# Low parts of split weights: a second use from DRAM, or a second subtraction

## The chip, the cores and the metric

One core of a Trainium2 chip (trn2) runs the whole program. The metric is the device time of one execution in microseconds (us), the median of several runs. The engines are named as the profile names them: PE is TensorE (PEld its weight loads), DVE is VectorE, ACT is ScalarE, POOL is GpSimd, and SP is SyncE, whose queue issues every DMA of this kernel.

## What is computed

Two token sequences, 512 and 256 long, 1024 channels wide, go through two layers that share one set of weights. In short:

```python
def encoder_trunk(x, mem, p):
    for l in range(2):
        xn = rmsnorm(x, p['norm_mix'][l])
        if l % 2 == 0:
            x = x + window_conv_mixer(xn, ...)               # layer 0: windowed attention and a gated conv
        else:
            x = x + rwkv7_bidir_time_mix(xn, ...)            # layer 1: six mixes of xn with its neighbours,
                                                             # r, k, v = products with three 1024x1024 weights,
                                                             # a forward and a backward recurrence over the tokens
        x = x + memory_cross_attention(rmsnorm(x), rmsnorm(mem), ...)
        gate, up = split(rmsnorm(x) @ p['ffn_wgu'][l])       # 1024 -> 2 x 2816
        x = x + (silu(gate) * up) @ p['ffn_wdown'][l]        # 2816 -> 1024
    return rmsnorm(x, p['norm_final'])
```

Everything is float32 and is held to float32's accuracy.

## The kernel before

**Split products.** A float32 matrix goes to TensorE as two parts in a rounded format (float32r): hi, which ScalarE rounds, and lo = value - hi. `mms` (L322 to L333) then issues three matmuls for every 128 rows of a weight: hi times the tokens' hi (L329), hi times their lo (L330), lo times their hi (L331). So every block of 128x128 weights that is used needs its hi and its lo in SBUF, in each place where it is used.

**Two ways to a split weight.** `wcols` (L250) serves the dense stages: one DMA brings 256 columns of up to 1024 rows as `wraw` (2 buffers, L262), ScalarE rounds each 128 columns into `whi` (L267) and VectorE subtracts into `wlo` (L268), 3 buffers each. `wtiles` (L276) serves the work in small pieces: a DMA brings 128 columns of 512 rows as `traw` (2 buffers, L287), ScalarE rounds into `thi` (L293), and the subtraction into `tlo` (L294, 3 buffers) is GpSimd's where the pieces run beside the scans, VectorE's elsewhere. One such piece of 4 x 128 rows is called a tile below; for 256 tokens TensorE makes 12 matmuls of it.

**The stages.** From about 760 us on: the last part of layer 0's feed-forward for the long sequence (`ffn` with `LATE`, hidden columns 8 to 21 of 22, by 128), then layer 1's r, k and v for the long sequence (`rwkv_in`, its inner function `full`), then, from 1278 us to about 2370 us, the recurrences (`mixer1_scan`). The recurrences are cut into 12 units; each unit is prepared (`prep`), has small triangular matrices inverted (`inverse`), is scanned (`scan`) and finished (`tail`): chains of small steps over TensorE, ScalarE, VectorE and GpSimd. They do not fill TensorE.

**The fill.** So dense work for the short sequence is woven in between: `fill` (L1388) makes, in order, the short sequence's hidden columns 8 to 21 of layer 0 (`ffn_small`, L391, with both its gate and up weights and its down weights), its low ranks (`small_low`), its v, k and r (`small_in`, L944), and then the keys and values of layer 1's memory and the output product (`mem_kv`, `rwkv_out`). The weights of `ffn_small` and of `small_in` are those that the dense stages used for the long sequence a few hundred us earlier; the weights of the other three are not.

**What sets the order.** A scheduler lays out the engines' queues at build time; each engine then runs its queue strictly in that order. Before the first scan, the fill's steps are placed beside `prep` and `inverse` by `weave`; inside a scan, `pour` releases some of the fill after a given matmul of the scan and not before:

```python
                todo[0] += rate[2 + u] / 24
                while todo[0] >= 1:
                    todo[0] -= 1
                    with tc.issue_after(last[0].ins):
                        next(fill, None)
```

SP's queue is in order too: a DMA that waits for its buffer holds up every DMA behind it, those of the scans included (`iok`, `ior`, `iov` at L1069, `w2r` at L1074, `v` at L1239).

Of the kernel before, what the change touches and what calls it, by code (L numbers as in the profile page):

```python
# [9 lines left out]
F32 = mybir.dt.float32  # L10
# [5 lines left out]
PSUM = bass.MemoryType.PSUM  # L16
# [9 lines left out]
# buffers of the dense layers' ring of big tiles  # L26
NBIG = 4
# how dense work is spread beside the scans (by step, before and after the long sequence's outputs are there)
FILL = ([1.2, 1.2] + [1.05] * 3 + [1.] * 3, [.9] * 2 + [1.] * 3 + [.5, 0.])
# rows of a weight between two points where the fill may pause, by tokens  # L30
PIECE = {256: 2, 512: 1, 768: 8}
# the hidden layer, by 128: the first layer's groups for all tokens and for the long sequence only, and the last layer's
# [5 lines left out]
class Net:  # L38
# [17 lines left out]
    def at(self, n):  # L56
        """The same, for tensors of n tokens."""
        f = copy.copy(self)
        f.W, f.seqs = n, ((0, n),)
        return f  # L60

    def sm(self, *shape):
        """A PSUM bank."""
        n = 1
        for s in shape:
            n *= s
        t = self.psm.tile([128, 512], F32, name="sm" if self.psm is not self.pmm else "mm")[:, :n]
        return t if len(shape) == 1 else t.rearrange("p (a b) -> p a b", b=shape[-1])
# [12 lines left out]
    def of(self, q):  # L81
        """The same, for one sequence."""
# [14 lines left out]
    def open_dense(self, small=3):  # L97
        """Pools for the dense layers."""
# [25 lines left out]
    def consts(self):  # L124
# [13 lines left out]
        # times the weights of the norm before  # L138
# [9 lines left out]
    # ---- residual stream, channel-major  # L148
# [8 lines left out]
    def rsqrt(self, v, n, eps, scale):  # L157
        """v [128, n] -> 1/sqrt(scale * v + eps), to float32's accuracy."""
# [17 lines left out]
    def spread(self, y, n):  # L176
        """y [128 tok, n token tiles] -> [128, n*128], the same row in every partition."""
# [12 lines left out]
    def square(self, m, x, acc=None, quick=False):  # L190
        """Adds the squares of x (channels 128*m on) per partition; quick: the last ones are left for rstd to add."""
# [12 lines left out]
    def rstd(self, acc, spread=True):  # L204
        """1/rms from the squares: in every partition, or (not spread) with the tokens on the partitions."""
# [22 lines left out]
    def split(self, src, g=None, tag="xs", bufs=16):  # L228
        """src (* g per channel) = hi + lo, both float32r."""
# [10 lines left out]
    def norm_in(self, name, l):  # L240
        """x*g split, and the squares for 1/rms (the products are scaled after)."""
# [6 lines left out]
    # ---- weights  # L248
    def wcols(self, w, r0, nk, c0, n):
        """Columns c0..c0+n of the rows r0..r0+128*nk of w, 128 at a time, as hi + lo by 128 rows."""  # L250
# [8 lines left out]
        for g0 in range(c0, c0 + n, W):  # L259
# [3 lines left out]
            for j in range(0, g, cw):  # L263
# [5 lines left out]
                for i in range(0, m, 128):  # L269
                    yield [(hi[:, k, i:i + 128], lo[:, k, i:i + 128]) for k in range(nk)]  # L270

    def wtiles(self, seq):
        """(hi, lo) of 128x128 blocks, of each (parts, rows[, factors of the rows]) of seq: 128 columns (in parts) of a
        matrix. Loads run ahead."""
# [3 lines left out]
        def load():  # L278
            for parts, nk, *scale in seq:
                for k0 in range(0, nk, 4):  # L280
# [8 lines left out]
                    for f in scale:  # L289
# [4 lines left out]
                    (nc.gpsimd if self.slots else nc.vector).tensor_sub(lo[:, :n], raw[:, :n], hi[:, :n].bitcast(F32))  # L294
# [8 lines left out]
    def abreast(self, ws, xs):  # L303
        """Some products of the same tokens, that take each of xs as it comes."""
# [6 lines left out]
    def mm(self, ps, w, xs, start=True, stop=True):  # L311
        """ps[out, tok] += w^T xs, in three passes."""
# [3 lines left out]
    def products(self, ps, pairs):  # L316
        """ps = the sum of a^T b over pairs (a, b), each in two parts, in three passes."""
# [17 lines left out]
    def ffn(self, l, given=None, groups=((0, 8), (8, 16), (16, 22)), keep=None, outs=None):  # L335
        """given: the norm's results, else they are left in normed. keep: gets the short sequence's hidden layer, which is not multiplied here."""
# [3 lines left out]
        pre = ahead(self.wcols(gu, 0, 8, c, 256), self.wcols(gu, 0, 8, DFF + c, 256))  # L340
# [8 lines left out]
        for h0, h1 in groups:  # L349
            hid = []  # L350
            for j in range(h0, h1, 2):
                if j != groups[0][0]:
                    pre = [self.wcols(gu, 0, 8, j * 128, 256), self.wcols(gu, 0, 8, DFF + j * 128, 256)]
# [27 lines left out]
            else:  # L381
                (self if keep is None else self.of(0)).ffn_down(l, h0, hid)

    def ffn_down(self, l, h0, hid):
        n = len(hid)
        for m, w in enumerate(self.wcols(self.a["ffn_wdown"][l], h0 * 128, n, 0, D)):
# [4 lines left out]
    def ffn_small(self, l, x, hid, part, h):  # L391
        """The same for few tokens, in small pieces, from tile h of the hidden layer on; what those before gave is in part.
        hid holds four tiles of the hidden layer."""
# [10 lines left out]
        for h0 in range(h, NH, 4):  # L404
            h1 = min(h0 + 4, NH)
            ws += [([gu[:, c:c + 128]], 8) for j in range(h0, h1) for c in (j * 128, DFF + j * 128)]
            ws += [([dn[h0 * 128:h1 * 128, c:c + 128]], h1 - h0) for c in range(0, D, 128)]
# [27 lines left out]
    # ---- cross-attention  # L435
    def mem_norm(self):
        """Both memories over their rms, to DRAM."""
# [17 lines left out]
    def mem_kv(self, l):  # L455
        """K [128 ch, 2*256] by 128 channels and V [128 tok, 4, 128] by 128 channels, of both memories, to DRAM."""
# [23 lines left out]
    def ca(self, l, kv):  # L480
# [3 lines left out]
        def load(h):  # L484
            """keys and values of a head, split"""
# [24 lines left out]
        def attend(h, st):  # L510
# [3 lines left out]
            def turn(p, t2):  # L514
                """keys on the partitions"""
# [62 lines left out]
    # ---- dilated-window attention and gated convolution  # L578
    def mixer0_tables(self, pool):
        """How many branches hold a pair of positions (by distance), and -1e30 where none does."""  # L580
# [25 lines left out]
    def mixer0(self):  # L606
# [23 lines left out]
        # the first products do not wait for the norm  # L630
# [26 lines left out]
        def turned(o):  # L657
            """values, token-major"""
# [10 lines left out]
        def attend(p, o):  # L669
# [3 lines left out]
            def turn(e, pT, hs, s0, t, n):  # L673
                """the probabilities of a tile of queries, keys on the partitions; values summed after two tiles"""
# [926 lines left out]
```

## Time and profile before

| what | us |
|---|---|
| median of 3 runs | 3186.92 |
| lowest and highest of them | 3182.41 and 3188.93 |
| the profiled execution, first to last instruction (its span) | 3179.3 |
| the profiled execution's own time | not listed apart from its span |
| busy in that span: PE | 2981.6 (94%) |
| DVE | 1948.5 (61%) |
| ACT | 1223.7 (38%) |
| POOL | 786.8 (25%) |

[...] Busy time of an engine includes time in which one of its instructions has begun and is held up. The stages differ, so shares over the whole span say little; the sections below go by stretches.

### The profile page before, as it was taken

What the parts mean: (1) busy time and instruction counts of PE and PEld (TensorE: products, weight loads), DVE (VectorE), ACT (ScalarE), POOL (GpSimd) and SP (SyncE); (2) the same over time, 40 slices, a digit from 0 to 9 for tenths busy, and PEclk for the clock granted to TensorE, in tenths of its full rate; (3) what the DMA queues carried; (4) which work ended last, traced back from release to release, by engine and by line L of the source; (5) the groups of instructions that cost most, each with busy time, mean ns of one, the idle gap of its engine ahead of it and who ended that gap; (6) DMA issues with size and microseconds to landing.
All of it is one profiled execution on the core that took longest, in us unless ns stands there. A gap on an engine that the chain in (4) does not pass through costs nothing. (4 is left out here: it accounts for less than half of the span.)

```text
span 3179.3 us, 49939 instructions
## 1 busy us (share of the span) xinstructions
PE 2981.6 (94%) x19984; PEld 2474.2 (78%) x19984; DVE 1948.5 (61%) x3492; ACT 1223.7 (38%) x2241; POOL 786.8 (25%) x753
## 2 busy tenths in 40 slices
PE   7999999999999899889888889999998999999997
PEld 6888788888888777677767767666677888888886
DVE  8678547464454684677697887666646564334244
ACT  3332434332222374454445565454435332122112
POOL 3112004020000201665466553343325120000001
PEclk9999999999999999889888998999999999999998
DMA  3123332112233435332232333222344211211211
GB/s 114 47 70 110 110 112 90 60 55 66 83 103 99 156 107 173 93 97 79 74 83 71 92 103 93 67 73 73 109 125 129 73 40 55 79 53 67 67 54 53
DMA packets 319880, 274.92 MB, mean 86 GB/s; under 512 B 37664, under 2 KB 283552, under 8 KB 319648
## 3 DMA queue, kind: packets, MB, share of 16 engines
q1 hardware_dynamic: 319648, 271.74, 27.0%
q8 instruction: 157, 2.57, 0.3%
q14 instruction: 75, 0.61, 0.1%
HBM read 234.46 MB, written 37.22 MB: 85 GB/s over the span
## 5 line engine op out<-in xcount | busy, mean ns | idle before, releaser
L329 PE MATMUL mm<-xs,whi 128*128 128x512 f32 x2128 | 752.6, 355 | 32.2 <-ACT whi L267 11.6
L330 PE MATMUL mm<-xs,whi 128*128 128x512 f32 x2128 | 753.4, 354 | 3.3 <-DVE xs L237 2.4
L331 PE MATMUL mm<-xs,wlo 128*128 128x512 f32 x2128 | 748.2, 352 | 3.8 <-DVE wlo L268 3.7
L267 ACT CAST whi<-wraw 128x1024 fp32r<-128x1024 f32 (+1 forms) x246 | 256.4, 1044 | 789.2 <-PE mm L330 757.3
L329 PEld LDWEIGHTS mm<-xs,whi 128*128 128x128 f32 x2128 | 403.1, 190 | 95.6 <-ACT whi L267 12.2
L201 POOL TENSOR_TENSOR acc<-acc,sq 128x768 f32<-128x768 f32 (+2 forms) x72 | 123.0, 1708 | 1412.7 <-ACT sq L198 1030.0
L331 PEld LDWEIGHTS mm<-xs,wlo 128*128 128x128 f32 x2128 | 401.6, 189 | 62.8 <-DVE wlo L268 5.5
L330 PEld LDWEIGHTS mm<-xs,whi 128*128 128x128 f32 x2128 | 402.9, 189 | 60.6 <-issue 3.3
L268 DVE TENSOR_TENSOR wlo<-wraw,whi 128x1024 fp32r<-128x1024 f32 (+1 forms) x246 | 314.0, 1279 | 158.7 <-ACT whi L267 150.8
L294 POOL TENSOR_TENSOR tlo<-traw,thi 128x512 fp32r<-128x512 f32 (+1 forms) x196 | 253.4, 1294 | 289.2 <-ACT thi L293 268.8
L330 PE MATMUL mm<-fb,thi 128*128 128x256 f32 (+1 forms) x720 | 242.6, 337 | 1.6 <-DVE fb L234 1.6
L329 PE MATMUL mm<-hid,whi 128*128 128x512 f32 (+1 forms) x528 | 186.9, 357 | 1.9 <-ACT hid L233 1.9
L330 PE MATMUL mm<-hid,whi 128*128 128x512 f32 (+1 forms) x528 | 188.2, 357 | 0.0
L329 PE MATMUL mm<-fb,thi 128*128 128x256 f32 x528 | 176.7, 335 | 11.0 <-ACT thi L293 10.9
L331 PE MATMUL mm<-hid,wlo 128*128 128x512 f32 (+1 forms) x528 | 186.7, 355 | 0.0
L331 PE MATMUL mm<-fb,tlo 128*128 128x256 f32 x528 | 164.0, 312 | 6.7 <-POOL tlo L294 6.5
L293 ACT CAST thi<-traw 128x512 fp32r<-128x512 f32 (+1 forms) x202 | 122.4, 608 | 121.1 <-PE mm L330 53.0
L369 DVE SCALAR_TENSOR_TENSOR u<-mm,rstd 128x768 f32<-128x768 f32 (+1 forms) x44 | 38.4, 873 | 211.6 <-PE mm L331 211.6
L1191 DVE TENSOR_TENSOR xr<-xr,lt 128x30 f32<-128x30 f32 (+4 forms) x360 | 156.0, 433 | 8.2
L330 PEld LDWEIGHTS mm<-fb,thi 128*128 128x128 f32 x720 | 152.7, 212 | 6.7 <-DVE fb L234 2.6
L1190 DVE TENSOR_TENSOR lt<-xr,lane 128x30 f32<-128x30 f32 (+4 forms) x360 | 149.5, 415 | 8.6
L389 DVE TENSOR_TENSOR x<-x,mm 128x512 f32<-128x512 f32 (+2 forms) x56 | 42.4, 762 | 175.9 <-PE mm L331 175.7
(366 smaller groups left out, 5995.5 us busy)
## 6 DMA issues: line engine op xcount, KB each, us to landing
wraw<-in_ffn_wgu_dram SPq DMA_DIRECT2D x44, 1024.0 KB, 4.9
wraw<-in_ffn_wdown_dram SPq DMA_DIRECT2D x23, 1024.0 KB, 5.0
traw<-in_ffn_wgu_dram SPq DMA_DIRECT2D x56, 256.0 KB, 3.0
wraw<-in_ab_w_in_dram SPq DMA_DIRECT2D x24, 512.0 KB, 3.6
wraw<-in_ca_wkv_dram SPq DMA_DIRECT2D x8, 1024.0 KB, 5.5
kvd<-kv SPq DMA_DIRECT2D x32, 256.0 KB, 2.0
kvr<-kvd SPq DMA_DIRECT2D x32, 256.0 KB, 2.6
wraw<-in_ca_wq_dram SPq DMA_DIRECT2D x8, 1024.0 KB, 5.2
```

The costliest lines, as they stand in the source:

```text
L201: nc.gpsimd.tensor_add(acc, acc, sq)
L267: nc.scalar.copy(hi[:, :, :m], raw[:, :, j:j + m])
L268: nc.vector.tensor_sub(lo[:, :, :m], raw[:, :, j:j + m], hi[:, :, :m].bitcast(F32))
L293: nc.scalar.copy(hi[:, :n], raw[:, :n])
L294: (nc.gpsimd if self.slots else nc.vector).tensor_sub(lo[:, :n], raw[:, :n], hi[:, :n].bitcast(F32))
L329: nc.tensor.matmul(ps[:, s0:s1], lhsT=wh, rhs=xh[:, s0:s1], start=start and k == 0, stop=False)
L330: nc.tensor.matmul(ps[:, s0:s1], lhsT=wh, rhs=xl[:, s0:s1], start=False, stop=False)
L331: nc.tensor.matmul(ps[:, s0:s1], lhsT=wl, rhs=xh[:, s0:s1], start=False, stop=stop and k == n - 1)
L369: nc.vector.scalar_tensor_tensor(u, pu, 0.5, rstd, op0=OP.mult, op1=OP.mult)
L389: self.nc.vector.tensor_add(self.x[m], self.x[m], ps)
L1190: nc.vector.tensor_mul(t, xr[:, m:, k:k + 1].to_broadcast([128, n, k]), ln[:, k:k + 1, 0:k].to_broadcast([128, n, k]))
L1191: nc.vector.tensor_add(xr[:, m:, 0:k], xr[:, m:, 0:k], t)
```

## The change

The first user of a weight keeps lo, the second user loads it:

- `wcols` gets a key (`keep`). With one, it issues a further DMA after each subtraction, from `wlo` to a DRAM tile `low` that belongs to that key and column. `ffn` passes a key where it is given the norm's results (the long sequence's columns 8 to 21: 28 gate and up columns and 16 down columns), `full` passes one for v, k and r (24 columns).
- `wtiles` takes such a tile as a third entry of a weight. With one, `tlo` is not computed: a DMA loads it from `low`. `ffn_small` and `small_in` pass them, for 56, 32 and 48 tiles. `thi` is rounded from `traw` as before.
- The other weights of the fill (low ranks, `mem_kv`, `rwkv_out`) keep GpSimd's subtraction.

```diff
+    def kept(self, key, nk):
+        if key not in self.lows:
+            self.lows[key] = self.lowd.tile([128, nk, 128], F32, name="low%d" % len(self.lows))
+        return self.lows[key]
-    def wcols(self, w, r0, nk, c0, n):
+    def wcols(self, w, r0, nk, c0, n, keep=None):
                 nc.vector.tensor_sub(lo[:, :, :m], raw[:, :, j:j + m], hi[:, :, :m].bitcast(F32))
                 for i in range(0, m, 128):
+                    if keep:
+                        nc.sync.dma_start(self.kept((*keep, (g0 + j + i) // 128), nk), lo[:, :, i:i + 128].bitcast(F32))
                     yield [(hi[:, k, i:i + 128], lo[:, k, i:i + 128]) for k in range(nk)]
...
-                    for f in scale:
+                    lows = scale if scale and len(scale[0].shape) == 3 else ()
+                    for f in () if lows else scale:
...
                     nc.scalar.copy(hi[:, :n], raw[:, :n])
-                    (nc.gpsimd if self.slots else nc.vector).tensor_sub(lo[:, :n], raw[:, :n], hi[:, :n].bitcast(F32))
+                    if lows:
+                        nc.sync.dma_start(lo[:, :n].bitcast(F32), lows[0][:, k0:k0 + n])
+                    else:
+                        (nc.gpsimd if self.slots else nc.vector).tensor_sub(lo[:, :n], raw[:, :n], hi[:, :n].bitcast(F32))
...
+        low = ("gu",) if given else None
...
-                (self if keep is None else self.of(0)).ffn_down(l, h0, hid)
+                (self if keep is None else self.of(0)).ffn_down(l, h0, hid, low and ("dn", h0))
...
-            wcs = self.wcols(a["rw_w" + c][0], 0, 8, 0, D)
+            wcs = self.wcols(a["rw_w" + c][0], 0, 8, 0, D, (c,))
...
-            col = lambda r, nk, m: ([w[r:r + 128 * nk, m * 128:m * 128 + 128]], nk)
+            col = lambda r, nk, m: ([w[r:r + 128 * nk, m * 128:m * 128 + 128]], nk, self.lows[c, m][:, r // 128:r // 128 + nk])
```

The order of the queues moves with it in three places.

SP's queue in the long sequence's feed-forward, where the raw weights are loaded (`wraw`) for `ffn`; before, a row "x8" is eight loads in a row:

```order
L262 DMA wraw<-in_ffn_wgu_dram 128x8x256 x6
L262 DMA wraw<-in_ffn_wdown_dram 128x8x256 x4
L262 DMA wraw<-in_ffn_wgu_dram 128x8x256 x8
L262 DMA wraw<-in_ffn_wdown_dram 128x8x256 x4
L262 DMA wraw<-in_ffn_wgu_dram 128x8x256 x6
```

and now, from the second of these rows on:

```order
L269 DMA wraw<-in_ffn_wdown_dram 128x8x256 x4
L269 DMA wraw<-in_ffn_wgu_dram 128x8x256 x2
L278 DMA low_7328<-wlo 128x1024
L278 DMA low_7336<-wlo 128x1024
L278 DMA low_7405<-wlo 128x1024
L269 DMA wraw<-in_ffn_wgu_dram 128x8x256
L278 DMA low_7440<-wlo 128x1024
L269 DMA wraw<-in_ffn_wgu_dram 128x8x256
```

One write of a low part stands in SP's queue for each column of 128, two for each load of raw weights, between the loads.

SP's queue where the fill begins beside the first unit's preparation, from the load of the scan's `v2` on, before:

```order
L1239 DMA v2_11924<-v00_8813 128x8x64
L287 DMA traw_10819<-in_ffn_wgu_dram 128x4x128
L287 DMA traw_10845<-in_ffn_wgu_dram 128x4x128
L287 DMA traw_10870<-in_ffn_wgu_dram 128x4x128
L287 DMA traw_10892<-in_ffn_wgu_dram 128x4x128
L287 DMA traw_10917<-in_ffn_wgu_dram 128x4x128
```

and now:

```order
L1255 DMA v2_12060<-v00_8901 128x8x64
L305 DMA tlo_10883<-low1_7336 128x512
L296 DMA traw_10955<-in_ffn_wgu_dram 128x4x128
L305 DMA tlo_10935<-low2_7405 128x512
L296 DMA traw_10981<-in_ffn_wgu_dram 128x4x128
L305 DMA tlo_10958<-low2_7405 128x512
L296 DMA traw_11006<-in_ffn_wgu_dram 128x4x128
L305 DMA tlo_10984<-low3_7440 128x512
```

Loads of raw and low parts alternate, and the low part of a tile stands behind the raw part of the tile after it. In the built program the load of `traw` waits for ScalarE's rounding (it waited for GpSimd's subtraction), and the load of `tlo` waits for the TensorE matmuls that used the buffer last.

TensorE's queue at the same place, the 6344th row of its order and those after it (`e` from `l0a` is a product of `prep`, L1057, now L1073; `g` are the first products of `inverse`, L1163; the others are the fill), before:

```order
L329 MATMUL mm_10916<-fb_10622,thi_10894 128x256
L330 MATMUL mm_10916<-fb_10622,thi_10894 128x256
L331 MATMUL mm_10916<-fb_10622,tlo_10895 128x256
L329 MATMUL mm_10916<-fb_10628,thi_10919 128x256
L330 MATMUL mm_10916<-fb_10628,thi_10919 128x256
L1057 MATMUL e_11048<-l0a_10535,w2r_10580 128x512
L1163 MATMUL g0_11193<-ar0_10838,bk0_10837 128x128
L1163 MATMUL g1_11194<-ar0_10838,bk0_10837 128x128
```

and now, in the same rows:

```order
L344 MATMUL mm_11052<-fb_10758,tlo_11031 128x256
L342 MATMUL mm_11052<-fb_10764,thi_11055 128x256
L343 MATMUL mm_11052<-fb_10764,thi_11055 128x256
L1073 MATMUL e_10978<-l0a_10671,w2r_10716 128x512
L344 MATMUL mm_11052<-fb_10764,tlo_11056 128x256
L342 MATMUL mm_11052<-fb_10770,thi_11055 128x256
L343 MATMUL mm_11052<-fb_10770,thi_11055 128x256
L344 MATMUL mm_11052<-fb_10770,tlo_11056 128x256
```

More of the fill stands in front of the first unit's products: the first `g` comes 58 rows later, and by the 80th matmul of the recurrences 130 more matmuls of the fill have gone before. By the 200th the difference is 6, and from there on the two orders hold the fill at the same places to within a tile or so.

## Rows read from the trace of the kernel before

**Rows 1.** The page: the span of the profiled execution.

```profile
span 3179.3 us, 49939 instructions
```

**Rows 2.** Stretches: us, then each engine's busy time (instructions), granted clock, DMA share, GB/s.

```profile
core 0: us, PE busy (x) PEld busy (x) DVE busy (x) ACT busy (x) POOL busy (x), PEclk, DMA share, GB/s
800.00:1000.00 200.00, 200.00 (x890) 165.78 (x889) 88.66 (x103) 49.86 (x58) 0.00 (x0) 1.00 0.29 94
```

**Rows 3.** Stretches of the recurrences: to the first scan's end, and while the fill shares weights.

```profile
1278.00:1425.00 147.00, 123.29 (x903) 101.86 (x902) 104.69 (x190) 72.76 (x147) 96.71 (x84) 0.89 0.31 90
...
1278.00:1920.00 642.00, 560.98 (x5183) 457.39 (x5184) 507.38 (x1079) 332.24 (x749) 369.57 (x385) 0.88 0.29 85
```

**Rows 4.** Waits of PE, 1278 to 1920 us: total us, times, longest us.

```profile
PE C L1254 <- DVE uv L1298: 20.1, 15, 3.4
PE C L1254 <- DVE S L1309: 14.7, 12, 2.5
PE mm L329 <- ACT thi L293: 6.0, 7, 1.4
...
PE mm L331 <- POOL tlo L294: 3.9, 2, 2.7
```

**Rows 5.** Groups of POOL, 1278 to 1920 us: xcount | busy us, mean ns | idle before it.

```profile
L294 POOL TENSOR_TENSOR tlo<-traw,thi 128x512 fp32r<-128x512 f32 (+1 forms) x144 | 186.6, 1298 | 148.0 <-ACT thi L293 129.7 <-PE C L1254 10.9 <-PE e L1023 3.5
```

**Rows 6.** Single lines of DVE, 1278 to 1920 us: ns min/median/max, first and last start.

```profile
L1191 DVE TENSOR_TENSOR xr<-xr,lt x210: 183/274/1396, 1343.4 to 1913.2; 128x30 f32<-128x30 f32 x14, 128x56 f32<-128x56 f32 x14, 128x78 f32<-128x78 f32 x14, 128x96 f32<-128x96 f32 x14
...
L1190 DVE TENSOR_TENSOR lt<-xr,lane x210: 174/271/1492, 1343.0 to 1913.0; 128x30 f32<-128x30 f32 x14, 128x56 f32<-128x56 f32 x14, 128x78 f32<-128x78 f32 x14, 128x96 f32<-128x96 f32 x14
...
L1298 DVE COPY uv<-C x47: 294/295/297, 1409.7 to 1915.7; 64x128 f32<-64x128 f32 x47
...
L1309 DVE TENSOR_TENSOR S<-C,Sd x72: 271/289/296, 1425.7 to 1918.6; 64x128 f32<-64x128 f32 x72
...
L169 DVE TENSOR_SCALAR rs_y<-rs_b x14: 163/172/1239, 1286.2 to 1877.5; 128x8 int32<-128x8 int32 x13, 128x2 int32<-128x2 int32 x1
```

**Rows 7.** Groups of DVE, 1278 to 1920 us: xcount | busy us, mean ns | idle.

```profile
L1191 DVE TENSOR_TENSOR xr<-xr,lt 128x30 f32<-128x30 f32 (+7 forms) x210 | 97.7, 465 | 4.6
L1190 DVE TENSOR_TENSOR lt<-xr,lane 128x30 f32<-128x30 f32 (+7 forms) x210 | 93.7, 446 | 4.7
```

**Rows 8.** Timeline around 1710 us: start us, duration us, engine, line [idle before].

```profile
1708.88 1.52 POOL L294 TENSOR_TENSOR tlo<-traw,thi 128x512 fp32r<-128x512 f32 x1
1709.19 1.24 DVE L169 TENSOR_SCALAR rs_y<-rs_b 128x8 int32<-128x8 int32 x1
...
1710.35 0.60 DVE L1309 TENSOR_TENSOR S<-C,Sd 64x128 f32<-64x128 f32 x2
...
1711.10 0.69 PE L1254 MATMUL C<-uv,G 64*64 64x64 f32 x8 [0.76 <-DVE S L1309]
```

**Rows 9.** DMA issues of the whole span: KB each, median us from issue to landing.

```profile
wraw<-in_ffn_wgu_dram SPq DMA_DIRECT2D x44, 1024.0 KB, 4.9
...
traw<-in_ffn_wgu_dram SPq DMA_DIRECT2D x56, 256.0 KB, 3.0
...
iok<-k SPq DMA_DIRECT2D x8, 256.0 KB, 2.7
```

**Rows 10.** Waits of SP's queue over the whole span.

```profile
SPq L262 <- DVE wlo L268: 1287.3, 119, 39.0
SPq L287 <- POOL tlo L294: 409.6, 144, 11.8
```

**Rows 11.** Timeline of PE: the first and the last of twelve matmuls of the fill.

```profile
1283.16 0.28 PE L329 MATMUL mm<-fb,thi 128*128 128x256 f32 x1
...
1284.46 0.28 PE L331 MATMUL mm<-fb,tlo 128*128 128x256 f32 x1
```

**Rows 12.** Lines that touch `traw`: ns min/median/max.

```profile
L293 ACT CAST thi<-traw x202: 389/618/637, 1083.5 to 2353.7; 128x512 fp32r<-128x512 f32 x97, 128x256 fp32r<-128x256 f32 x4
...
L287 SPq DMA_DIRECT2D traw<-in_ffn_wgu_dram x56: 367/368/539, 1234.3 to 1586.7; - x56
```

**Rows 13.** GpSimd's subtractions to the first scan's end: ns min/median/max.

```profile
L294 POOL TENSOR_TENSOR tlo<-traw,thi x42: 1262/1282/2187, 1283.1 to 1423.6; 128x512 fp32r<-128x512 f32 x42
```

More of the change, by code (lines that the diff above doesn't have):

```diff
@@ L339, in ffn @@
         c = 128 * groups[0][0]
-        pre = ahead(self.wcols(gu, 0, 8, c, 256), self.wcols(gu, 0, 8, DFF + c, 256))
+        low = ("gu",) if given else None
+        pre = ahead(self.wcols(gu, 0, 8, c, 256, low), self.wcols(gu, 0, 8, DFF + c, 256, low))
         first = None
@@ L352, in ffn @@
                 if j != groups[0][0]:
-                    pre = [self.wcols(gu, 0, 8, j * 128, 256), self.wcols(gu, 0, 8, DFF + j * 128, 256)]
+                    pre = [self.wcols(gu, 0, 8, j * 128, 256, low), self.wcols(gu, 0, 8, DFF + j * 128, 256, low)]
                 wg, wu = pre
@@ L381, in ffn, with ffn_down @@
             else:
-                (self if keep is None else self.of(0)).ffn_down(l, h0, hid)
-    def ffn_down(self, l, h0, hid):
+                (self if keep is None else self.of(0)).ffn_down(l, h0, hid, low and ("dn", h0))
+    def ffn_down(self, l, h0, hid, low=None):
         n = len(hid)
-        for m, w in enumerate(self.wcols(self.a["ffn_wdown"][l], h0 * 128, n, 0, D)):
+        for m, w in enumerate(self.wcols(self.a["ffn_wdown"][l], h0 * 128, n, 0, D, low)):
             ps = self.pmm.tile([128, self.W], F32, name="mm")
@@ L405, in ffn_small @@
             h1 = min(h0 + 4, NH)
-            ws += [([gu[:, c:c + 128]], 8) for j in range(h0, h1) for c in (j * 128, DFF + j * 128)]
-            ws += [([dn[h0 * 128:h1 * 128, c:c + 128]], h1 - h0) for c in range(0, D, 128)]
+            ws += [([gu[:, c:c + 128]], 8, self.lows["gu", c // 128]) for j in range(h0, h1) for c in (j * 128, DFF + j * 128)]
+            g0 = max(g for g, _ in LATE if g <= h0)
+            ws += [([dn[h0 * 128:h1 * 128, c:c + 128]], h1 - h0, self.lows["dn", g0, c // 128][:, h0 - g0:h1 - g0])
+                   for c in range(0, D, 128)]
         ws = self.wtiles(ws)
@@ L1516, in go @@
     n.xsave = [[dram.tile([128, s1 - s0], F32, name=f"xsave{q}{m}") for m in range(KT)] for q, (s0, s1) in enumerate(SEQS)]
+    n.lowd, n.lows = dram, {}
     n.consts()
```

## The prediction

> **What bounds the kernel now.** The page first, for the span: 3179.3 us [rows 1]; the median of the runs, 3186.92 us, lies 7.6 us above it, and the forecast is the median plus the sum below. Next the busy time by stretches, since one share over the whole span mixes stages. In the dense stage from 800 to 1000 us PE is busy 200.00 of 200 us at clock 1.00, for 890 matmuls, 0.225 us each [rows 2]: nothing but PE work counts there. From 1278 to 1920 us, where the recurrences run and the fill works with weights that were split before, it is different: PE is busy 560.98 of 642 us, so idle 81 us, and its clock is granted at 0.88, which costs about 0.12 x 642 = 77 us more [rows 3]. No other engine is full: DVE is busy 507 us (79%), POOL 370 us (58%). This stretch is a web of chains between engines, so I read the waits of PE there: the long ones end on DVE, 20.1 us on the copy L1298 and 14.7 us on the state sum L1309; on ScalarE's `thi` it waits 6.0 us and on GpSimd's `tlo` only 3.9 us [rows 4]. So the subtraction that goes is hardly waited for itself. What it does to DVE is the question.
>
> **GpSimd and VectorE hold each other up.** The group of L294 has 144 subtractions, 186.6 of POOL's 370 us, 1298 ns each [rows 5]. Single lines of DVE in the same stretch vary wildly: L1191 takes 183 to 1396 ns, L1190 174 to 1492, and L169, on 8 columns, 172 ns as a rule and 1239 at worst; the copy and the sum that read PSUM, L1298 and L1309, never leave 271 to 297 ns [rows 6]. The timeline shows one case: a subtraction runs from 1708.88 to 1710.40 us, L169 begins at 1709.19 and ends at 1710.43, just behind it, the state sum L1309 starts only then, and PE stands 0.76 us until it is done [rows 8]. That is the path by which a subtraction reaches the end of the kernel.
>
> **The change, part by part.**
>
> *Writes of the low parts*, 68 DMAs (60 of 512 KB, 8 of 384 KB) in the dense stages. I cost them at nothing. No engine computes for them; they read `wlo` behind the subtraction that makes it, which the next raw load in SP's queue waits for anyway (1287.3 us in all, over the span [rows 10]), so the queue stands where it stood. A raw load lands in 4.9 us [rows 9] and feeds two columns, 48 matmuls or 10.8 us of PE [rows 2]: that is the cover. If it were gone and each of the 34 raw loads concerned came 1 us late, it would cost 34 us.
>
> *Subtractions removed.* 136 go; four start before 1278 us, so 132 of the 144 in the group, 171 us or 46% of POOL's time in the stretch. The gain on DVE is bounded from rows. On L1191 the mean is 465 ns against a median of 274, on L1190 446 against 271 [rows 6, 7]: 210 x (0.191 + 0.175) = 77 us above the median on these two lines, and 46% of that is 36 us. This is the lower end; if the rest of DVE's 507 us suffered as these 191 us do, it would be 95 us, the upper end. I take 55 us, nearer the lower end, because the lines on PSUM do not suffer at all.
>
> [...]
>
> *What passes to the end.* Between nothing (DVE gets idle instead) and all of it. I take half, 28 us: DVE is the engine that PE waits for most, but not the only one. The clock: 81 us of idle PE go with 77 us of lost clock, so 28 us less idle could return up to 27 us; I take 14 us.
>
> *The start.* Before, a tile came every 147 / 42 = 3.5 us to the first scan's end [rows 3, 13], with PE idle 24 of 147 us. A raw buffer was then free only after landing (3.0 us), rounding (0.6) and subtraction (1.3); now after the first two, which with 0.4 us of issue is about 4 us for two tiles [rows 9, 12]. So the fill can run ahead, and the order now has 130 more of its matmuls, 130 x 0.118 = 15 us of PE [rows 11], in front of the 80th one of the recurrences. Bounds: 15 us gained if all of that falls into idle time, 15 us lost if the recurrences' chain is only pushed back and nothing returns. I take a gain of 4 us.
>
> *Loads of the low parts*, 136 DMAs on SP's queue, 132 x 0.37 = 49 us more of issue [rows 12], on a queue that waited 409.6 us for the subtraction [rows 10]. About 35 MB more in 642 us, 54 GB/s on top of 85, at a DMA share of 0.29 [rows 3]: no bound by itself. The new wait is the load's own: `tlo` has three buffers, so a load can go out when the matmuls of the tile three before are done, and needs 0.4 + 2.7 us (the landing of `iok`, also 256 KB with long rows [rows 9]), while two tiles of back-to-back fill last only 2 x 12 x 0.118 = 2.8 us [rows 11]. Behind a load that waits for PE stand SP's loads for the scans, and behind a matmul that waits for `tlo` stands the whole of PE's queue. Bounds: nothing where scan matmuls lie between the tiles (the mean distance is 642 / 144 = 4.5 us), 0.3 us for each of 132 tiles, 40 us, if all ran back to back. I take 7 us.
>
> Sum: 0 - 28 - 14 - 4 + 7 = -39 us, so **3148 us**.
>
> **The rivals.**
>
> *Late loads (slower).* The landing time in the sum is that of a lone load; now raw and low loads alternate. From 256 to 1024 KB the landing grows from 3.0 to 4.9 us [rows 9], 0.63 us for 256 KB, so two at once need 3.7 us against 2.8: 0.9 us short for each tile in a burst. At the start, where the new order has 40 tiles nearly in a row, that is 36 us on PE's queue, and with a fifth of the relief passing (11 us) the time is 3187 + 36 - 11 = 3212 us. It decides from about 3 us of issue to landing on. For it: the order has no slack for a longer landing. Against it: before, the raw buffers and a busy POOL made the fill slower still.
>
> [...]
>
> *Hidden anyway (no change).* The relief goes into DVE's own waits: what PE waits for, L1298 and L1309, runs at a constant time and waits in turn for PE and ScalarE. Then 3185 us. Against it: L1309 behind L169 in the timeline [rows 8].
>
> *All of it passes (much faster).* 55 us of relief and more, the 9.9 us on `thi` and `tlo`, and half of the clock's 77 us: 55 + 10 + 38 = 103 us, 3084 us. For it: from 1278 us on DVE is 79% busy with these chains. [...]
>
> That the change does not do what it says I exclude: the hidden columns and the weights that the fill loads are those for which the dense stages have keys. The fill's other subtractions stay.
>
> **How the numbers follow.** Forecast 0.50, its own range 3125 to 3170 us; all passes 0.15; hidden 0.14; late loads 0.21. A measurement tells about 0.2%, 6.4 us, from no change. Faster by more than that: 0.50 + 0.15 = 0.65; within it 0.14; slower 0.21. The range goes from 3100 us, halfway between the forecast and the case where all passes, to 3205 us, which takes in most of the late loads.
>
> **What would show it.** Right: no L294 of these tiles on POOL, POOL near 200 us between the same points; means of L1190 and L1191 near 350 ns; DVE's busy time in the stretch about 55 us less; PE's idle time there below 60 us with a clock above 0.88; the first g products a few us later, the first scan's end no later. Wrong: PE waiting for `tlo` loads for more than 20 us; landings above 3.5 us; the dense stage from 800 to 1000 us with PE below 199 us; or DVE relieved as said and PE as idle as before.

## The result and the profile after

The changed kernel takes **3128.23 us** (median of 4 runs, 3127.19 to 3129.72) against 3184.66 us for the kernel before beside it (4 runs, 3169.79 to 3188.93): a ratio of 0.984, 95% interval 0.9819 to 0.9861, 56 us faster. A second set of runs gave 3126.91 against 3177.65 us, 0.9837 (0.9817 to 0.9857). The forecast was 3148 us, in a range of 3100 to 3205: the direction is right, the time lies inside the range, the gain is larger than the 39 us predicted. The range is wide (it also holds no change and a slower kernel); of the forecast's own range, 3125 to 3170, the time lies at the fast edge.

The head of the page, then the busy time by stretches (columns as in [rows 2, 3]):

```profile
span 3127.9 us, 50086 instructions
...
PE 2967.1 (95%) x19984; PEld 2465.7 (79%) x19984; DVE 1863.9 (60%) x3492; ACT 1223.7 (39%) x2241; POOL 608.6 (19%) x617
```

```profile
1278.00:1868.00 590.00, 541.82 (x5233) 444.40 (x5233) 430.54 (x1081) 335.42 (x756) 196.42 (x253) 0.91 0.50 151
1278.00:1425.00 147.00, 128.99 (x905) 106.92 (x906) 85.66 (x191) 74.09 (x149) 39.96 (x44) 0.83 0.53 168
800.00:1000.00 200.00, 200.00 (x890) 165.88 (x889) 88.87 (x104) 50.08 (x58) 0.00 (x0) 1.00 0.50 173
```

What took 642 us before [rows 3] now takes 590. DVE is busy 431 in place of 507 us, POOL 196 in place of 370, PE stands idle 48 in place of 81 us, and its clock is granted at 0.91 in place of 0.88. The dense stage is as full as it was [rows 2].

Where in the stretch the time went is read from progress. I count PE's instructions of the recurrences. The 400th starts at 1425.4 us in both kernels. The 3600th starts at 1931.0 us before and at 1878.9 us after; from there on the distance stays at 50 us or so (the 6400th at 2334.0 and 2282.4). So in these two profiles everything was gained between the 400th and the 3600th, with 1200 matmuls of the fill between them in both. These are the windows of exactly this work, first of the kernel before, then of the changed one:

```profile
1425.40:1931.00 505.60, 447.86 (x4418) 363.45 (x4414) 404.53 (x893) 266.54 (x618) 276.16 (x306) 0.89 0.29 85
```

```profile
1425.40:1878.90 453.50, 423.33 (x4416) 345.15 (x4416) 347.00 (x893) 265.98 (x617) 158.69 (x211) 0.93 0.49 146
```

The same 893 instructions of DVE take 57.5 us less. Of the 52.1 us gained, 27.5 are idle time of PE (505.6 - 447.9 = 57.7 against 30.2 us) and the remaining 24.6 are PE's busy time for the same matmuls, which is the clock: against the 1.00 of the dense stage, 0.11 x 505.6 = 55.6 us lost before, 0.07 x 453.5 = 31.7 after.

The groups of DVE that answer to [rows 7] (L1190 and L1191 are now L1206 and L1207; the copy L1298 is L1314, the sum L1309 is L1325), PE's longest waits as in [rows 4] (L331 is now L344), both from 1278 to 1868 us, and SP's waits and DMA issues of the whole span that answer to [rows 9, 10]:

```profile
L1206 DVE TENSOR_TENSOR lt<-xr,lane 128x30 f32<-128x30 f32 (+7 forms) x210 | 73.3, 349 | 4.6
L1207 DVE TENSOR_TENSOR xr<-xr,lt 128x30 f32<-128x30 f32 (+7 forms) x210 | 70.4, 335 | 4.6
```

```profile
PE C L1270 <- DVE uv L1314: 15.9, 11, 3.2
PE mm L344 <- DMA tlo<-low: 7.5, 7, 2.3
PE g L1230 <- DVE rs_t L171: 4.9, 1, 4.9
PE C L1270 <- DVE S L1325: 3.4, 2, 2.7
```

```profile
SPq L269 <- DVE wlo L275: 1081.9, 86, 39.0
SPq L278 <- DVE wlo L275: 218.6, 60, 11.6
SPq L305 <- PE mm L344: 209.1, 84, 29.5
SPq L296 <- POOL tlo L307: 132.0, 44, 10.9
```

```profile
tlo<-low SPq DMA_DIRECT2D x128, 256.0 KB, 3.2
low<-wlo SPq DMA_DIRECT2D x60, 512.0 KB, 3.1
...
traw<-in_ffn_wgu_dram SPq DMA_DIRECT2D x56, 256.0 KB, 3.8
...
iok<-k SPq DMA_DIRECT2D x8, 256.0 KB, 4.0
```

The two substitution lines fell from 446 and 465 ns to 349 and 335. The wait on the state sum fell from 14.7 to 3.4 us, that on the copy from 20.1 to 15.9; the rest of the idle time saved is spread over smaller waits. The new wait, for loads of the low parts, is 7.5 us. SP now waits for PE (L305, 209.1 us) where it waited for GpSimd (409.6 us [rows 10], now 132.0). The loads of raw parts take longer to land than before, 3.8 us in place of 3.0, and those of `iok` 4.0 in place of 2.7 [rows 9].

### The profile page after: what moved, and what is told of

It is laid out like the page before. It is cut to its first block, busy times and chain, and to the rows that moved or that the text cites. A ratio compares the mean times of both kernels' runs of the same rounds, so it can differ in the third digit from the quotient of the medians.

```text
span 3127.9 us, 50086 instructions
## 1 busy us (share of the span) xinstructions
PE 2967.1 (95%) x19984; PEld 2465.7 (79%) x19984; DVE 1863.9 (60%) x3492; ACT 1223.7 (39%) x2241; POOL 608.6 (19%) x617
## 5 line engine op out<-in xcount | busy, mean ns | idle before, releaser
L343 PE MATMUL mm<-xs,whi 128*128 128x512 f32 x2128 | 756.1, 355 | 3.1 <-DVE xs L237 2.2
L344 PE MATMUL mm<-xs,wlo 128*128 128x512 f32 x2128 | 750.4, 353 | 2.1 <-DVE wlo L275 2.1
L343 PEld LDWEIGHTS mm<-xs,whi 128*128 128x128 f32 x2128 | 404.6, 190 | 60.8 <-issue 3.3
L344 PEld LDWEIGHTS mm<-xs,wlo 128*128 128x128 f32 x2128 | 403.5, 190 | 60.7 <-DVE wlo L275 3.7
L343 PE MATMUL mm<-fb,thi 128*128 128x256 f32 (+1 forms) x720 | 236.3, 328 | 0.0
L343 PE MATMUL mm<-hid,whi 128*128 128x512 f32 (+1 forms) x528 | 187.8, 356 | 0.0
L344 PE MATMUL mm<-hid,wlo 128*128 128x512 f32 (+1 forms) x528 | 186.4, 354 | 0.0
L342 PE MATMUL mm<-fb,thi 128*128 128x256 f32 x528 | 170.3, 323 | 7.0 <-ACT thi L303 5.1
L344 PE MATMUL mm<-fb,tlo 128*128 128x256 f32 x528 | 157.9, 301 | 10.2 <-DMA tlo<-low 5.2
L343 PEld LDWEIGHTS mm<-fb,thi 128*128 128x128 f32 x720 | 147.2, 204 | 5.1 <-issue 1.2
L1206 DVE TENSOR_TENSOR lt<-xr,lane 128x30 f32<-128x30 f32 (+4 forms) x360 | 130.4, 362 | 8.4
L342 PE MATMUL mm<-fa,thi 128*128 128x512 f32 (+1 forms) x304 | 132.5, 437 | 0.2 <-DVE fa L448 0.2
L1207 DVE TENSOR_TENSOR xr<-xr,lt 128x30 f32<-128x30 f32 (+4 forms) x360 | 124.7, 346 | 8.4
```

Of the source, the lines that this page charges most:

```text
L342: nc.tensor.matmul(ps[:, s0:s1], lhsT=wh, rhs=xh[:, s0:s1], start=start and k == 0, stop=False)
L343: nc.tensor.matmul(ps[:, s0:s1], lhsT=wh, rhs=xl[:, s0:s1], start=False, stop=False)
L344: nc.tensor.matmul(ps[:, s0:s1], lhsT=wl, rhs=xh[:, s0:s1], start=False, stop=stop and k == n - 1)
L1206: nc.vector.tensor_mul(t, xr[:, m:, k:k + 1].to_broadcast([128, n, k]), ln[:, k:k + 1, 0:k].to_broadcast([128, n, k]))
L1207: nc.vector.tensor_add(xr[:, m:, 0:k], xr[:, m:, 0:k], t)
```

## The experiments

**Theory A**: GpSimd's subtraction holds VectorE up, and VectorE's delay reaches PE. Its rivals: **B**, GpSimd's own work in the recurrences queued behind the subtractions; **C**, the fill got its low parts or its raw buffers too late. The first four kernels put work back on GpSimd whose result nothing reads, in the branch that loads a low part, while `tlo` still comes from DRAM:

```diff
                     if lows:
                         nc.sync.dma_start(lo[:, :n].bitcast(F32), lows[0][:, k0:k0 + n])
+                        nc.gpsimd.tensor_sub(raw[:, :n], raw[:, :n], hi[:, :n].bitcast(F32))
```

> The changed kernel with one more GpSimd instruction for each kept tile: the old subtraction, written back into the raw tile, which nothing reads again. The low parts still come from DRAM, so no matmul waits for GpSimd. Theory A (the subtraction holds VectorE up): about 3180 us, 3170 to 3190, with the means of the two substitution lines back above 430 ns. Rival B (GpSimd's own later work in the recurrences queues behind the subtractions): also near 3180, but with those means near 350 ns. Rival C (the fill gained because tlo was late): the time stays at 3128 to 3138 us.

Measured: 3185.19 us, ratio to before 1.0023 (1.0006 to 1.004). The whole gain is gone, and the two lines run long again (1278 to 1935 us):

```profile
L1208 DVE TENSOR_TENSOR xr<-xr,lt 128x30 f32<-128x30 f32 (+7 forms) x210 | 93.7, 446 | 4.8
L1207 DVE TENSOR_TENSOR lt<-xr,lane 128x30 f32<-128x30 f32 (+7 forms) x210 | 91.2, 434 | 4.6
```

That is what A expects, where B expected them near 350. The part of C about late low parts falls: no matmul waits for this subtraction.

The second kernel has, in that place, two times `nc.gpsimd.memset(raw[:, :n], 0.0)`:

> The changed kernel with two fills of the raw tile with zeros on GpSimd for each kept tile, behind its rounding: GpSimd is busy and the raw buffer is held as before, but no instruction there reads SBUF. The zeroed tile is read by nothing. Theory A: 3128 to 3140 us, VectorE's substitution lines near 350 ns. Rival B, and the rival that the raw buffer's earlier release is what counts: back towards 3185 in proportion to GpSimd's added time, 3150 or more if the two take over 0.6 us together.

Measured: 3111.28 us, ratio 0.9811 (0.9762 to 0.986), its runs from 3108.0 to 3140.1, and in a second set 3123.71 us, 0.9838 (0.981 to 0.9866): both below the window of theory A, on the fast side, and far from that of B. The two lines, 1278 to 1868 us:

```profile
L1208 DVE TENSOR_TENSOR lt<-xr,lane 128x30 f32<-128x30 f32 (+7 forms) x210 | 72.8, 346 | 4.6
L1209 DVE TENSOR_TENSOR xr<-xr,lt 128x30 f32<-128x30 f32 (+7 forms) x210 | 71.4, 340 | 4.4
```

GpSimd is nearly as busy, the raw buffer is held, and nothing is lost. B falls, and with it the part of C about raw buffers. The windows from the 400th to the 3600th instruction of the recurrences, of the dummy subtraction and of the zero fills:

```profile
1436.10:1934.70 498.60, 445.64 (x4414) 360.63 (x4413) 405.07 (x891) 264.54 (x615) 278.06 (x305) 0.89 0.44 131
```

```profile
1418.00:1864.80 446.80, 412.69 (x4418) 332.88 (x4416) 355.50 (x895) 268.81 (x621) 250.48 (x397) 0.95 0.50 148
```

POOL is busy 278 and 250 us (276 in the kernel before), DVE 405 and 356. Of the dummy subtraction's loss 45 us lie in this stretch (498.6 against 453.5 us); the 400th instruction comes 10.7 us later as well, after 18.7 us of waits for `thi`. The zero fills cause 16.7 us of such waits there and no delay, so holding the raw buffer is not by itself what costs; what makes up the 10.7 us stays open. The timelines show what happens to VectorE. First the kernel with the dummy subtraction (start, duration, engine, line):

```profile
1449.94 1.30 POOL L306 TENSOR_TENSOR traw<-traw,thi 128x512 f32<-128x512 f32 x1 [0.67 <-POOL Sd L1344]
1450.14 1.21 DVE L1207 TENSOR_TENSOR lt<-xr,lane 128x78 f32<-128x78 f32 x1
...
1452.42 1.26 POOL L306 TENSOR_TENSOR traw<-traw,thi 128x512 f32<-128x512 f32 x1 [1.18 <-ACT thi L303]
1452.52 1.28 DVE L1207 TENSOR_TENSOR lt<-xr,lane 128x96 f32<-128x96 f32 x1
1453.84 0.26 DVE L1208 TENSOR_TENSOR xr<-xr,lt 128x96 f32<-128x96 f32 x1
1454.12 0.29 DVE L1315 COPY uv<-C 64x128 f32<-64x128 f32 x1
...
1454.47 0.34 PE L1271 MATMUL C<-uv,BT 128*64 128x64 f32 x4 [2.14 <-DVE uv L1315]
```

Twice an instruction of the substitution (`lt` and `xr`), which takes 0.23 to 0.26 us undisturbed, starts 0.1 to 0.2 us behind the start of a subtraction and ends 0.1 us behind its end. The second time the copy to `uv` comes late by that, and PE stands 2.14 us. Under a zero fill the same lines run in 0.25 to 0.26 us:

```profile
1338.83 0.26 DVE L1208 TENSOR_TENSOR lt<-xr,lane 128x96 f32<-128x96 f32 x1
1339.03 0.53 POOL L306 MEMSET traw<- 128x512 f32 x1 [3.15 <-ACT thi L303]
1339.13 0.26 DVE L1209 TENSOR_TENSOR xr<-xr,lt 128x96 f32<-128x96 f32 x1
1339.42 0.25 DVE L1208 TENSOR_TENSOR lt<-xr,lane 128x92 f32<-128x92 f32 x1
```

Two more kernels change the kind and the length of the dummy. One copies with one input, `nc.gpsimd.tensor_copy(raw[:, :n], hi[:, :n].bitcast(F32))`; the other subtracts on `[:, :n, :64]`, half of each tile's columns:

> The changed kernel with a GpSimd copy of the rounded tile into the raw tile, which nothing reads again, for each kept tile: one SBUF input in place of two. Theory A in its strict form (only instructions with two SBUF inputs on GpSimd hold VectorE up): 3115 to 3140 us, the substitution lines near 350 ns. Any reading of SBUF by GpSimd holds VectorE up: the lines above 400 ns and 3150 us or more.

> The changed kernel with the dummy subtraction on half of each tile's columns, some 0.7 us of GpSimd each, less than the 1.05 us of the two zero fills. Theory A: about half of the 57 us comes back, 3148 to 3165 us, the substitution lines near 390 ns. If GpSimd's time alone counted: nearer the changed kernel than the zero fills are.

Measured: the copy 3135.69 us, 0.9871 (0.985 to 0.9892); the half subtraction 3158.42 us, 0.992 (0.9888 to 0.9952), its runs from 3126.5 to 3164.0. The groups of the copy's kernel, then of the half subtraction's, 1278 to 1868 us:

```profile
L306 POOL COPY traw<-thi 128x512 f32<-128x512 f32 x123 | 80.5, 657 | 168.7 <-ACT thi L303 160.5 <-issue 3.6 <-POOL Sd L1344 2.4
...
L1208 DVE TENSOR_TENSOR xr<-xr,lt 128x30 f32<-128x30 f32 (+7 forms) x210 | 80.0, 381 | 4.7
L1207 DVE TENSOR_TENSOR lt<-xr,lane 128x30 f32<-128x30 f32 (+7 forms) x210 | 78.0, 371 | 4.9
```

```profile
L306 POOL TENSOR_TENSOR traw<-traw,thi 128x256 f32<-128x256 f32 x115 | 90.2, 786 | 145.2 <-ACT thi L303 134.2 <-issue 5.0 <-POOL Sd L1344 2.4
...
L1207 DVE TENSOR_TENSOR lt<-xr,lane 128x120 f32<-128x120 f32 (+8 forms) x184 | 70.3, 382 | 4.2
L1208 DVE TENSOR_TENSOR xr<-xr,lt 128x120 f32<-128x120 f32 (+8 forms) x183 | 68.2, 372 | 3.8
```

So the strict form, that only two inputs hold VectorE, is refuted by the lines, though the time fell in its window: the copy raises the two lines, from 349 and 335 ns to 371 and 381. The other form missed too, since it asked for more than 400 ns and 3150 us. From the starts in the traces, a line `lt<-xr,lane` that starts while the dummy runs takes 1073 ns on average under the whole subtraction (29 cases), 679 under the half (24), 510 under the copy (28) and 263 under a zero fill (64), against 332 to 351 for those that start while none of the first three kinds of dummy runs. The times follow the length of the dummies that read: 0.66, 0.79 and 1.31 us each give 9, 31 and 58 us over the changed kernel's 3127; 1.05 us that read nothing give none. The 31 is rough, since that kernel's runs spread over 37 us. Why the copy costs less for its length than the half subtraction I did not settle.

**What VectorE's time is worth.** Here VectorE does the subtraction (the load replaced by `nc.vector.tensor_sub(lo[:, :n], raw[:, :n], hi[:, :n].bitcast(F32))`, the writes left out):

> The subtraction of the kept tiles done by VectorE in place of GpSimd, nothing kept in DRAM. VectorE gets 136 instructions of some 0.6 us more, about 80 us, in place of what GpSimd's subtraction held it up. Theory A: near the time before, 3175 to 3200 us, since 80 us of work replace 77 us of holding up. Rival B: GpSimd's queue is free as in the changed kernel, so clearly faster than before, 3140 to 3165 us.

Measured: 3243.41 us, 1.0198 (1.0168 to 1.0229), slower than both theories said. The stretch of equal work, and the new group:

```profile
1433.90:1982.40 548.50, 501.17 (x4418) 406.61 (x4416) 412.54 (x983) 267.66 (x616) 160.87 (x210) 0.79 0.27 78
```

```profile
L305 DVE TENSOR_TENSOR tlo<-traw,thi 128x512 fp32r<-128x512 f32 (+1 forms) x115 | 91.8, 800 | 24.9 <-ACT thi L303 24.4
```

Against the changed kernel DVE works 65.5 us more and the stretch is 95 us longer. Idle time of PE is only 17 us of it (47.3 against 30.2); the other 78 are PE's busy time (501.2 against 423.3), since the clock was granted at 0.79 in place of 0.93. It is also 43 us longer than the same stretch of the kernel before, where DVE worked nearly as much (404.5 us) and PE stood idle 10 us more (57.7): only the clock is lower, 0.79 against 0.89. The trace shows four stretches of 38 to 44 us at 0.50 in it (from 1485, 1584, 1792 and 1881 us on); in the kernel before the longest there is 20.5 us. So neither DVE's total nor PE's idle time tells the price alone; what brings these stretches on was not tested.

**The writes alone** (`if lows:` made `if False:` at the load, so that the fill subtracts as before):

> The low parts are written to DRAM as in the changed kernel, but the fill subtracts on GpSimd as before: the price of the 68 writes alone. If they are free, as I costed them: 3180 to 3190 us. If they delay raw loads: up to 34 us more, 3190 to 3220 us.

Measured: 3185.04 us, 1.0014 (0.9995 to 1.0033). The writes are free within what can be measured.

**Which tiles.** A counter of the kept tiles splits them at the 43rd, which is the last that the fill uses before the first scan's end (`if lows and self.tiles > 43:`, and `<= 43`):

> The first 43 kept tiles, those up to the first scan's end, are subtracted on GpSimd as before; the other 93 are loaded. If the whole gain comes behind the first scan, as the progress of the two traces says: 3115 to 3135 us. If the start's relief is needed too: 3145 us or more (two thirds of the gain at most, 93 of 136).

> The other half: the first 43 kept tiles are loaded, the other 93 are subtracted on GpSimd as before. If the start gives nothing: 3178 to 3190 us. If each tile gives the same: 57 x 43 / 136 = 18 us less than before, about 3165 us.

Measured: late tiles loaded 3144.87 us, 0.9891 (0.9854 to 0.9927); start tiles loaded 3174.93 us, 0.9989 (0.9971 to 1.0007). Each lies between the two times that its text gave, that of the late tiles right at the edge of the second (3145). The start alone gives nothing that can be measured. The late tiles give most: 1.1% of 3177 us, or 35 us, against 1.6%, or 52 us, for all tiles in their second set; in the profile their stretch takes 467.6 us, 14 more than in the changed kernel, with DVE at 359 and the clock at 0.91. The two parts, 35 us and 2, do not add up to the whole; what the early loads change behind the start stays open.

**The start and the clock.** In the changed kernel the fill has done 480 of its first 516 matmuls by the 200th instruction of the recurrences, at 1387 us (before: 386, at 1391 us). The windows around it:

```profile
1278.00:1380.00 102.00, 89.37 (x619) 75.86 (x618) 67.72 (x153) 56.66 (x113) 31.44 (x34) 0.96 0.71 225
1380.00:1390.00 10.00, 4.62 (x120) 4.08 (x122) 6.34 (x20) 5.64 (x10) 1.83 (x3) 0.55 0.16 48
1390.00:1425.00 35.00, 35.00 (x176) 26.99 (x174) 11.59 (x18) 11.79 (x27) 6.69 (x8) 0.50 0.11 33
```

PE stands idle more than half of the 10 us up to 1390, at a granted mean of 0.55, and then works 35 us without a pause at 0.50. A matmul of 128x256 of the fill (L343) takes 416 ns there (median of 12), and 281 ns from 1425.4 to 1520 us, where the granted clock is 1.00. The zero fills had no such stretch in their first profile, so I took it for the cause of their lower time (theory D) and limited them to the first 43 tiles (in the branch of the load, `if self.tiles <= 43:` before the two fills):

> The changed kernel with GpSimd's two fills with zeros only on the first 43 kept tiles, those that the fill uses up to the first scan's end. There the changed kernel's fill runs ahead, is used up near 1383 us, and PE then idles and runs at a granted clock of 0.50 to 1425 us (22 us lost). Theory D (the run ahead costs the start its gain through the clock): no such stretch, the clock of 1278 to 1425 us above 0.92, and the time near that of the kernel with zero fills on all tiles, 3105 to 3118 us. Rival (that kernel gained later, by some other way): 3124 to 3132 us, as the changed kernel.

> The changed kernel itself, on the chip of the runs beside it, to set it against the one with zero fills on all tiles: 3120 to 3140 us by every theory.

> The kernel with two zero fills on GpSimd for each kept tile once more. If slowing the run ahead is worth something: 3105 to 3118 us, at least 0.3% below the changed kernel beside it. If its lower time was the spread between executions: within 0.3% of the changed kernel.

Measured: 3138.46 us for the start only, 0.9864 (0.982 to 0.9907), its runs from 3121.5 to 3146.3; side by side, 3126.91 us for the changed kernel and 3123.71 us for the zero fills (3116.4 to 3144.4). The start-only kernel missed both of its windows, on the slow side, and theory D falls as an account of the time. The stretch at 0.50 is real: it stood in all five profiles in which the fill had 480 matmuls done by the 200th instruction, for 44 to 48 us in each. The start-only kernel did not have it (its clock from 1278 to 1425 us is 0.97), yet its 400th instruction came only 5 us earlier (1420.3), and its median is no lower. The zero fills' second profile had such a stretch from 1405 to 1445 us. So no kernel is shown to beat the changed one: the difference between the zero fills and it, 3 us side by side, is less than the spread of their runs.

**The tail.** The output weight's low parts kept as well, written by the fill and loaded in the 24 tiles near 2320 to 2360 us, where GpSimd subtracts (of the edit, the lines that name the key; the write and the load in `wtiles` are left out here):

```diff
...
-        for m, w in enumerate(self.wcols(self.a["rw_wo"][0], 128 * k0, len(zs), 0, D)):
+        for m, w in enumerate(self.wcols(self.a["rw_wo"][0], 128 * k0, len(zs), 0, D, ("wo",))):
```

> The changed kernel that also keeps the low parts of the output weight: the fill writes them after its subtraction, and the 24 tiles of the tail near 2320 to 2360 us load them. There GpSimd's subtraction of 1.3 us for each tile stands in the chain that ends last. If it bounds the tail: 10 to 25 us less than the changed kernel, 3103 to 3118 us. If the raw loads bound it: 3124 to 3132 us.

Measured: 3142.57 us, 0.9884 (0.9853 to 0.9916): against both expectations some 15 us slower than the changed kernel. (Only 8 of the 24 tiles are whole; the other 16 have half as many rows, and GpSimd's subtraction there takes 0.74 us, not 1.3.) At the 6400th instruction of the recurrences this kernel is still 3.6 us ahead (2278.8 against 2282.4 us). PE's waits from 2278 to 2420 us of this kernel, then those of the changed one from 2282 us:

```profile
PE mm L347 <- DMA tlo<-low: 9.7, 7, 4.9
PE e L1042 <- ACT bc L1039: 3.9, 1, 3.9
PE sm L538 <- DVE p L561: 2.0, 1, 2.0
PE mm L345 <- ACT thi L304: 1.5, 3, 0.5
```

```profile
PE mm L344 <- POOL tlo L307: 4.7, 3, 2.5
PE mm L342 <- ACT thi L303: 4.4, 3, 3.2
```

And the windows of equal work from the 6400th instruction on, to the end of these tiles and a little into the attention behind them, in the same order:

```profile
2278.80:2374.50 95.70, 77.59 (x570) 62.34 (x569) 33.87 (x75) 40.54 (x81) 18.32 (x16) 0.86 0.59 191
2374.50:2435.80 61.30, 57.77 (x353) 50.76 (x352) 37.94 (x64) 24.82 (x48) 21.37 (x14) 0.97 0.26 74
```

```profile
2282.40:2369.00 86.60, 74.50 (x571) 60.74 (x570) 38.85 (x76) 41.02 (x82) 44.72 (x41) 0.90 0.49 154
2369.00:2425.10 56.10, 55.84 (x351) 49.55 (x350) 34.44 (x63) 24.53 (x47) 19.52 (x13) 1.00 0.26 81
```

The same work takes 14.3 us longer: PE is idle 9.3 us more, and busy 5.0 us more at the lower clock. The waits for the tiles themselves are only 2 us longer, 11.2 us (9.7 for loads, 1.5 for `thi`) against 9.1: the loads of low parts come no sooner than GpSimd's subtraction did. The other 7 us of idle time are a wait for `bc`, a step of the last unit, and three short waits in the attention behind. So the rival *late loads* shows here as far as the loads gained nothing, and in a small part of the loss; why the other waits arose was not tested.

## Why the prediction was right, and where its sizes were off

- *Writes at nothing*: right. 1.0014 (0.9995 to 1.0033) alone, and PE busy 200.00 of 200 us. SP's wait for `wlo` only moved: 1287.3 us at the raw loads before, 1081.9 there and 218.6 at the writes now.
- *DVE relief of 55 us, bounds 36 and 95*: 76.8 us over the whole stretch, 57.5 of it behind the first scan, where all of the gain lies. **This size was too small by 22 us**, though inside its bounds. Theory A is shown by the dummy subtraction, which takes the gain back, and by the zero fills, which do not. The single cases show it on VectorE's side: 1073, 679 and 510 ns under a subtraction, a half and a copy, 263 under a fill that reads nothing. On GpSimd's side the trace of before has single cases: the subtraction that starts at 1423.59 us, 0.1 us behind the start of L1101 on VectorE, which runs to 1424.71, takes 2.19 us against a median of 1.28 [rows 13]. The 132 subtractions removed took 171 us of POOL's time, and the relief of DVE was 77 us, 45% of that. In the trace of before, 59 of the 420 starts on the two substitution lines fall within a subtraction, 29 on L1190 and 30 on L1191; these take 1092 and 1081 ns on average, the others 343 and 362. Whether the number of such starts sets the size of the relief was not tested by itself.
- *Half passes as idle time, 28 us*: 27.5 us behind the first scan, 48% of the 57.5 us there. The share is right; that the microseconds agree too is luck, since they were worked out for the whole stretch, where 33 of 77 us (43%) came out and the part at the start bought no time.
- *The clock, 14 us*: **the term of the sum that was mis-sized most**. I let half of the lost clock that goes with the idle time return; behind the first scan 24 us returned, about as much as the idle time itself. It is no fixed price: VectorE's own subtraction had 17 us more idle time with 78 us of slower matmuls, and at the start the clock fell (0.89 to 0.83) while idle time fell (23.7 to 18.0 us).
- *The start, a gain of 4 us within 15 either way*: none. PE idle fell from 23.7 to 18.0 us up to 1425 us, and the clock fell from 0.89 [rows 3] to 0.83 in the same stretch; the 400th instruction starts at 1425.4 us in both.
- *Late loads, 7 us*: 7.5 us of waits, all of them before 1425 us. What they cost at the end can't be told apart: the start came out even with them in it, so this term and the start's gain are both nothing in the bookkeeping, and that 7 and 7.5 agree is no proof of the term. With the clock's 10 us and these 7, less the start's 4, the sum of -39 becomes the -52 us of the stretch; the profiled spans differ by 51.4 us.
- *Rivals.* "Hidden anyway" fell, as the state sum's wait shows (14.7 to 3.4 us). "All passes" fell: of 77 us of relief 33 became idle time saved. "Late loads" did not come in the fill, although its condition did: I had it decide from about 3 us to landing on, and the low parts took 3.2. Its 36 us assumed 40 tiles nearly in a row, each 0.9 us short; PE waited seven times, 7.5 us in all. So the price was wrong, not the landing time.
- *The range.* Its lower end, 3100 us, is not halfway between 3148 and 3084, as the text says; halfway is 3116. The measured times lie above either.
- *The signs named beforehand*: POOL 196 us (about 200), the two lines at 349 and 335 ns (near 350), idle 48 us (below 60) at a clock of 0.91 (above 0.88), waits for loads 7.5 us (below 20), the first `g` 4.7 us later, the first scan's end no later: all as said. DVE's fall of 77 us was named as 55. One sign of being wrong came as well: landings above 3.5 us, at the raw loads (3.8) and at `iok` (4.0), though not at the low parts (3.2). PE hardly waited for them, so it was a poor sign.

## What to carry to other kernels

An engine that is hardly waited for (here 3.9 us for GpSimd's `tlo` [rows 4]) can still set the time by what it does to its neighbour (here 58 us, with the dummy subtraction): look at one instruction form of the neighbour, and if its mean is far above its median (465 against 274 ns) while its PSUM-reading lines are constant (271 to 297 ns [rows 6, 7]), find out under what it runs long. Moving the work to that neighbour is no cure (3243 us); moving it to DMA was one in the fill, where the changed kernel issued a load of a low part every 4.4 us (3127), and gained nothing in the tail, where GpSimd's subtractions of these tiles came every 2.0 us in the changed kernel (3143); that the distance is the reason was not tested. And where PE's clock is granted below the 1.00 of the dense stage (0.88 here [rows 3]), do not price an idle microsecond at one: in the stretch of the gain the clock gave back about as much as the idle time did (24 and 27.5 us), while in other stretches the two did not move together (78 and 17 us with VectorE's own subtraction).

## What the runs showed of the hardware

A GpSimd copy of 128x512 with one input also holds up VectorE's `lt<-xr,lane`, which has two inputs (510 ns on average for those that start under it, 350 for the others); a zero fill of the same tile does not (263 ns). In the changed kernel PE was busy 4.62 of the 10 us up to 1390 us; the clock was then granted at 0.50 up to 1425 us, although PE never paused in those 35 us. Runs of one program can lie 1.2% apart: those of the half subtraction go from 3126.5 to 3164.0 us.
